# A hybrid decoder block on one core: the first loads cut into smaller pieces, the first projection by k tile, later constants

## The chip, the cores and the metric

The kernel runs on one core of one Trainium2 chip. The metric is device time in microseconds (us), from the first to the last instruction of a launch and what lies around them. Before the change the median of three runs is 2488.16 us (2482.79 to 2489.18).

## What is computed

One decoder block over 16 learned meta tokens and 512 tokens of width 2048, all in float32:

- n = RMSNorm(h), with h the meta tokens and x one after the other.
- proj = n @ w_in, 7200 columns: q, k, v, gate z, decay and write-strength columns of a gated delta rule (8 heads of 128), and q, k, v, gate, gate-rank columns of gated linear attention (4 heads).
- q, k, v of the delta rule go through a causal convolution over 4 tokens (conv_w) and SiLU; then both attentions, each with its own norm and gate.
- h = h + mixed @ w_out; h = h + (silu(n2 @ w_gate) * (n2 @ w_up)) @ w_down; a final RMSNorm; the meta tokens are dropped.

## The kernel before, in words

**Dense products.** They are a stream of granules of weights. A granule of w_in is 4 k tiles (of 128 rows) by 256 columns, 512 KB. It is loaded into a tile `raw` (2 buffers), split by ScalarE into a high part `wh` (a cast to float32r) and by VectorE into a low part `wl` = raw - wh (3 buffers each), and used in 8 units. A unit (`unit` in `job`, line 450) is one k tile by 128 columns: six products of 258 or 264 columns, high by high, high by low, low by high, for two halves of the tokens. Four granules (16 k tiles) are one projection of 256 columns; its two times two results stay in four banks of PSUM (`psD`, 4 buffers) until they are scaled by R1 (1 / the norm of each token) on VectorE. The first projection is the queries of heads 0 and 1. In a granule all four k tiles of the first 128 columns come before those of the second.

**The stream.** `run_granules` (line 252) splits granule i+1 and issues loads up to granule i+3 at the head of granule i, then issues the units; after unit 0 (after unit 5 while the start's `hooks` last) it splits granule i+2. The weight loads are issued from ScalarE's queue, but the first two from SyncE's (lines 1551, 1553).

**The start.** SyncE loads x in 16 pieces of 128 tokens by 512 columns (256 KB), with the first two granules of weights between them. ScalarE's queue loads the rows of three weight vectors into `rowsA` (lines 290 to 292: attn_norm_w, ffn_norm_w, conv_w) and the meta tokens (line 294). TensorE runs nine products of ones (`warm`), transposes `rowsA`, and VectorE copies the result to `colA`, which holds the norm's weights by column (`aw`, `fw`) and the taps of the convolution. `n_tile(k)` (line 409) transposes a k tile of x with four TensorE transposes; ScalarE writes its high part, scaled by `aw`, VectorE the low part. `n_meta` does that for all k tiles of the meta tokens. Tiles 0 to 3 and `n_meta` come ahead of the first unit; tiles 4 to 15 are hooks, one after every second unit, and between them hooks with the squares of x and the meta tokens on ScalarE (20 of them), from which R1 is made. The hook after the last of these, `start`, comes after unit 24 of the first projection: it issues the sums, `t_norm` (R1: VectorE sums, ScalarE roots, a VectorE product, two TensorE products, a VectorE copy), `t_consts` (masks, then seven small loads on SyncE's queue, a transpose, the flag "consts") and the tasks of the four pairs of heads.

**The work beside the products.** Every engine runs in the order of the text. Convolutions, attentions and gates are generators cut into steps (`tick`, `step`, lines 152 to 167); a step is issued between two units once, by the kernel's own rough count of nanoseconds (`Paced`, `clock`), what the step before has issued is done. So a task that starts later falls between other units. `t_conv` (line 608) begins when its projection's flag is set, with a ScalarE product by a column of `colA`. A pair of heads (`t_pair`, line 651) solves its triangular blocks on VectorE with tiles `bl` and `y`; `y` is loaded from a small DRAM tile `idd` by three SyncE loads (line 738), and `need` (line 176) is what the stream calls when it can't go on without a flag.

Of the kernel before, what the change touches and what calls it, by code (L numbers as in the profile page):

```python
# [59 lines left out]
class Clock:  # L60
    """where the engines stand by a rough count (ns) of what has been issued to them"""
    now = 0.0    # TensorE
    last = None  # the engine of the last instruction
    dma = 0.0    # transfers of the current step
    chain = 0.0  # end of what the current step has issued, as if each instruction waited for the one before


class Paced:
    """an engine whose instructions are counted"""
# [28 lines left out]
def tile_block(  # L98
# [47 lines left out]
    # Engines run in the order of this text: work beside the dense products is cut into steps  # L146
    # (generators) that are issued between units of the dense products, once what the step before
    # has issued is done, and while the other engines keep up.
# [28 lines left out]
    def need(ok):  # L177
        """what the dense products cannot go on without"""
        stop = clock.now + 1e6
        while not ok():  # L180
            assert clock.now < stop
            clock.now += 200
            tick()

    hooks = []  # steps of the start, one after each unit
# [6 lines left out]
    def free(n):  # L192
        """the last use of n tiles of the arena has been issued"""
        live[0] -= n

    def room(n, spare):
        """tiles of the arena for a step; the dense products keep some spare"""
        while live[0] + n > AR - spare:
            yield
# [7 lines left out]
    def acquire(tag, n=1):  # L207
        """tiles that are held across steps: at most n holders at a time"""
        while held.get(tag, 0) >= n:
            yield  # L210
        held[tag] = held.get(tag, 0) + 1
# [5 lines left out]
    # granule: (loads [(weights AP, first column of the tile)], k tiles, columns, units, after)  # L217
# [17 lines left out]
    def split(i):  # L235
        grow(i)
        while state["split"] <= min(i, len(granules) - 1):
# [4 lines left out]
            if "split" in g:  # L242
                g["w"] = g["split"](raw)
                continue
            last_split()
# [6 lines left out]
    def run_granules(a, b):  # L252
        for i in range(a, b):
            g = granules[i]
            split(i + WB - 2)
            fetch(i + WB + RAW - 2)
            for n, u in enumerate(g["units"]):
                u(*g["w"])
                clock.chain = clock.now
                if n == (5 if hooks else 0):  # L260
# [29 lines left out]
    A.dma_start(out=rowsA[96:112], in_=attn_w.rearrange("o (r c) -> (o r) c", c=P))  # L290
    A.dma_start(out=rowsA[112:128], in_=ffn_w.rearrange("o (r c) -> (o r) c", c=P))
    A.dma_start(out=rowsA[0:96], in_=conv_w.rearrange("o i (t c) -> (o i t) c", c=P))
    for g in range(2):
        A.dma_start(out=mt[g][0:NM], in_=meta[:, 1024 * g:1024 * g + 1024])
    aw = colA[:, 96:112]
# [3 lines left out]
    # more constants, off the critical path  # L299
# [14 lines left out]
    def t_consts():  # L314
# [8 lines left out]
        # persistent: the columns that no product fills stay zero  # L323
# [3 lines left out]
        def blocks(dst, step, w):  # L327
            """dst[p, n, :] = 1 for step * n <= p < step * n + w"""
# [8 lines left out]
        # score masks of the hierarchical levels: columns of the right halves alone  # L337
# [3 lines left out]
        V.memset(rowsB, 0.0)  # L341
        SP.dma_start(out=rowsB[0:1], in_=gdn_w)
# [4 lines left out]
        # rows 3i + g of the identity for row group g, the same for every block  # L347
# [4 lines left out]
        PE.transpose(out=cps[:, 0:P], in_=rowsB, identity=ident)  # L352
        V.tensor_copy(out=colB, in_=cps[:, 0:8])
        flags.add("consts")

    def rstd_of(dst, ssq, n):
        """dst = (ssq / n + eps) ** -0.5"""
# [3 lines left out]
    def row_bcast(*jobs):  # L361
        """dst[128, t n] = the columns [n, t] along the free axis, on every partition"""
# [27 lines left out]
    def load_x(g):  # L390
        for t in range(NT):
            SP.dma_start(out=xq[g][t], in_=xv[:, t, 512 * g:512 * g + 512])
# [48 lines left out]
    w_in_v = w_in[0].rearrange("(k p) c -> p k c", p=P)  # L441

    def job(loads, evac, full=True, cols=256, mw=P, kk=4, after=None, mid=None, begin=None, hv=None):
        """projection of cols columns; evac(ct, psum AP, token slice); after(), mid() once the last, the
        lower k tiles are done"""
# [23 lines left out]
        for g in range(KT // kk):  # L469
            granules.append(dict(  # L470
                loads=[(w_in_v[:, kk * g:kk * g + kk, c0:c0 + w], c) for c0, w, c in loads], kk=kk, cols=cols,
                units=[unit(ct, kk * g + i, i) for ct in range(nct) for i in range(kk)],
# [20 lines left out]
    def ab_job():  # L493
        """32 columns: the high and the low parts of the weights side by side, rows 0-31 and 32-63 of abT"""
# [69 lines left out]
    def t_silu(t, w):  # L564
        """t * sigmoid(t), sigmoid(t) = exp(min(t, 0) - log(1 + exp(-|t|))): one table set, no overflow"""
# [14 lines left out]
    def squares(t, w):  # L580
        """t * t as a pair of float32r tiles that add up to it"""
# [11 lines left out]
    def gdn_job(j, gi):  # L593
# [9 lines left out]
        # the convolution of the first query reaches back to token NM - 3; float32r products take even columns  # L603
# [4 lines left out]
    def t_conv(j, gi, h, res):  # L608
        """conv + silu of a head's q, k or v; q and k normalized as well; no query of a meta token is asked for"""
        t = 8 * gi + 2 * j + h  # L610
        yield from until(("pre", j, gi))
# [1073 lines left out]
```

## Time and profile before

| | us |
|---|---|
| median of 3 runs | 2488.16 |
| lowest, highest run | 2482.79, 2489.18 |
| span of the profiled execution (core 0) | 2485.6 |
| TensorE busy in it | 2435.0 (98%) |
| VectorE busy | 1581.9 (64%) |
| ScalarE busy | 992.4 (40%) |

The profile is one execution of the same program. Its page gives busy times and the chain of work that ended last; the trace behind it can be asked for waits (who waited for whom), for busy times in stretches, and for the instructions in order of time. A row of the timeline shows start, duration, engine, operation, output and inputs, the number of like instructions that are merged, and in brackets how long the engine sat idle before and what ended that. PE is TensorE, DVE VectorE, ACT ScalarE, SP SyncE; ACTq and SPq are the queues from which they issue transfers.

### The profile page before, as it was taken

The page shows a single profiled execution, that of the slowest core. Times are in us where ns is not written, and L with a number is a line of the kernel's source. Part 1 is how long each engine was busy: PE and PEld are TensorE (multiplying, and loading weights), DVE is VectorE, ACT ScalarE, POOL GpSimd, SP SyncE. Part 2 cuts the span into 40 slices and gives each one's busy share as a digit, 9 for nine tenths or more (in the row PEclk, how much of TensorE's full clock was granted, in tenths as well). Part 3 has the DMA queues.
Part 4 walks back from the last instruction along what each step waited for, and adds up shares of the span by engine and source line. Part 5 has one row for each costly group of instructions (what it writes and reads, how often), then busy time and mean ns, then how long its engine had stood idle before and what let it go on. Part 6 is the DMA issues. An engine that isn't in the chain of part 4 may idle for free.

```text
span 2485.6 us, 39777 instructions
## 1 busy us (share of the span) xinstructions
PE 2435.0 (98%) x16512; PEld 2249.4 (90%) x16512; DVE 1581.9 (64%) x2598; ACT 992.4 (40%) x1515; POOL 129.3 (5%) x220
## 2 busy tenths in 40 slices
PE   9989898999999999999999999999999999999998
PEld 8989898788899888889999999999999988888887
DVE  5567566647544555369888888888888854334344
ACT  6545342533343554344444444444444433222213
POOL 1011110112202100000000000000000000000000
PEclk9999999899999999999999999999999999999999
DMA  4322232222222246343333333334334475434321
GB/s 144 87 79 79 66 81 64 73 71 78 56 61 69 78 143 200 122 136 111 117 122 120 118 120 119 119 111 126 113 119 125 126 257 183 130 96 144 106 81 68
DMA packets 237412, 274.43 MB, mean 110 GB/s; under 512 B 32625, under 2 KB 180344, under 8 KB 237104
## 3 DMA queue, kind: packets, MB, share of 16 engines
q10 hardware_dynamic: 198256, 232.49, 30.6%
q1 hardware_dynamic: 38976, 39.42, 5.0%
q8 instruction: 129, 2.11, 0.4%
q14 instruction: 51, 0.42, 0.1%
HBM read 246.61 MB, written 25.25 MB: 109 GB/s over the span
## 4 chain that ended last, share of the span: by engine, by line
PE 90%; SPq 3%; DMA 3%; DVE 2%; ACT 1%; issue 0%; ACTq 0%; DVEq 0%
PE ub L92 35%; PE dn L92 21%; PE dwn L92 19%; PE wo L92 7%; SPq L92 3%; PE sc L92 1%; DMA dy<-y 1%; PE py L92 1%; DVE acc L92 1%; DMA y<-idd 1%; PE hT L92 1%; PE lo L92 1%; PE pk L92 1%; DMA raw<-in_w_in_dram 1%; PE pz L92 1%
## 5 line engine op out<-in xcount | busy, mean ns | idle before, releaser
L92 PE MATMUL ub<-pl,sh 128*128 128x256 f32 x2816 | 550.6, 282 | 0.0
L92 DVE TENSOR_TENSOR wl<-raw,wh 128x1024 fp32r<-128x1024 f32 x224 | 275.6, 1230 | 372.9 <-ACT wh L92 371.5
L92 PEld LDWEIGHTS ub<-pl,sh 128*128 128x128 f32 x2816 | 436.9, 191 | 0.6 <-issue 0.5
L92 PE MATMUL ub<-pl,ah 128*128 128x256 f32 x2112 | 424.0, 282 | 0.0
L92 ACT CAST wh<-raw 128x1024 fp32r<-128x1024 f32 x224 | 234.9, 1049 | 416.6 <-PE dwn L92 212.4
L92 PE MATMUL ub<-pl,sl 128*128 128x256 f32 x1408 | 397.6, 282 | 0.0
L92 PE MATMUL dwn<-wh,pl 128*128 128x512 f32 x1280 | 396.0, 390 | 0.0
L92 PEld LDWEIGHTS ub<-pl,ah 128*128 128x128 f32 x2112 | 327.4, 191 | 0.0
L92 PE MATMUL dn<-nA,wh 128*128 128x264 f32 (+2 forms) x1472 | 304.4, 321 | 0.0
L92 PE MATMUL ub<-pl,al 128*128 128x256 f32 x1056 | 298.2, 282 | 0.0
L92 PE MATMUL dn<-nB,wh 128*128 128x264 f32 (+2 forms) x1472 | 296.4, 314 | 0.4 <-DVE nB L92 0.3
L92 PEld LDWEIGHTS dwn<-wh,pl 128*128 128x128 f32 x1280 | 240.2, 188 | 52.0 <-DVE pl L92 0.3
L92 ACT CAST sh<-us 128x1024 fp32r<-128x1024 f32 x176 | 185.0, 1051 | 237.3 <-DVE us L92 234.3
L92 PEld LDWEIGHTS ub<-pl,sl 128*128 128x128 f32 x1408 | 268.2, 190 | 0.0
L92 PE MATMUL dwn<-wl,pl 128*128 128x512 f32 x640 | 249.9, 390 | 0.0
L92 ACT CAST ah<-raw 128x768 fp32r<-128x768 f32 x176 | 147.3, 837 | 228.9 <-PE ub L92 223.1
L92 PEld LDWEIGHTS dn<-nA,wh 128*128 128x128 f32 x1472 | 223.2, 194 | 15.9 <-issue 3.2
L92 PEld LDWEIGHTS dn<-nB,wh 128*128 128x128 f32 x1472 | 218.2, 189 | 14.2 <-issue 1.2
L92 DVE TENSOR_TENSOR sl<-us,sh 128x1024 fp32r<-128x1024 f32 x176 | 214.6, 1219 | 1.8 <-ACT sh L92 1.8
L92 PEld LDWEIGHTS ub<-pl,al 128*128 128x128 f32 x1056 | 201.2, 191 | 0.0
L92 PE MATMUL dn<-nA,wl 128*128 128x264 f32 (+2 forms) x736 | 183.4, 313 | 0.0
L92 PE MATMUL dn<-nB,wl 128*128 128x264 f32 (+2 forms) x736 | 180.4, 309 | 0.0
(286 smaller groups left out, 3281.1 us busy)
## 6 DMA issues: line engine op xcount, KB each, us to landing
raw<-in_w_in_dram ACTq DMA_DIRECT2D x110, 512.0 KB
raw<-in_w_gate_dram ACTq DMA_DIRECT2D x88, 512.0 KB
raw<-in_w_up_dram ACTq DMA_DIRECT2D x88, 512.0 KB
raw<-in_w_down_dram ACTq DMA_DIRECT2D x80, 512.0 KB
raw<-in_w_out_dram ACTq DMA_DIRECT2D x32, 512.0 KB
actd<-up SPq DMA_DIRECT2D x22, 512.0 KB
jk<-actd ACTq DMA_DIRECT2D x41, 256.0 KB
x<-in_x_dram SPq DMA_DIRECT2D x16, 256.0 KB
```

Source lines behind the costliest of these rows:

```text
L92: return f(*args, **kw)
```

## The change

- The rows of attn_norm_w go alone into a tile `rowsC` of 16 rows, first on ScalarE's queue; a transpose of 16 rows gives `aw`, which is now a tile of its own. ffn_norm_w and conv_w are loaded into `rowsA` in `t_consts`, on SyncE's queue, and transposed there beside `rowsB`; `colA` is complete only then, and `t_conv` waits for "consts".
- The first 512 columns of x are loaded as two halves of 256 columns: first the four left halves, then the four right ones. The first granule of weights goes to ScalarE's queue, behind the meta tokens, as two loads of 2 k tiles. The second granule comes on SyncE's queue after the right halves, ahead of the rest of x.
- The first granule is split k tile by k tile (`split0`): k tiles 0 and 1 ahead of the first unit, 2 and 3 as hooks (in place of the squares after tiles 2 and 3).
- `n_meta` comes before tile 0; only tiles 0 and 1 come ahead of the first unit, tiles 2 and 3 are hooks. With 28 hooks ahead of it in place of 24, `start` comes after unit 28.
- In the four granules of the first projection both halves of the columns of a k tile come one after the other.
- In granule 0 the split of granule 1 comes before the hook of unit 4 and the loads of granules 2 and 3 before that of unit 5, in place of the head of the granule.
- Comments are dropped.

```diff
 run_granules:
-            split(i + WB - 2)
-            fetch(i + WB + RAW - 2)
+            first = i == 0 and len(hooks) > 0
+            if not first:
+                split(i + WB - 2)
+                fetch(i + WB + RAW - 2)
             for n, u in enumerate(g["units"]):
                 u(*g["w"])
                 clock.chain = clock.now
-                if n == (5 if hooks else 0):
+                if first:
+                    if n == 4:
+                        split(i + WB - 2)
+                    if n == 5:
+                        fetch(i + WB + RAW - 2)
+                elif n == (5 if hooks else 0):
                     split(i + WB - 1)
 constants:
-    A.dma_start(out=rowsA[96:112], in_=attn_w...)
-    A.dma_start(out=rowsA[112:128], in_=ffn_w...)
-    A.dma_start(out=rowsA[0:96], in_=conv_w...)
-    for g in range(2):
-        A.dma_start(out=mt[g][0:NM], in_=meta[...])
-    aw = colA[:, 96:112]
+    rowsC = const.tile([16, P], F32, name="rowsC")
+    aw = const.tile([P, 16], F32, name="aw")
 t_consts:
         V.memset(rowsB, 0.0)
+        V.memset(rowsA, 0.0)
+        SP.dma_start(out=rowsA[112:128], in_=ffn_w...)
+        SP.dma_start(out=rowsA[0:96], in_=conv_w...)
...
         PE.transpose(out=cps[:, 0:P], in_=rowsB, identity=ident)
+        PE.transpose(out=cps[:, P:2 * P], in_=rowsA, identity=ident)
         V.tensor_copy(out=colB, in_=cps[:, 0:8])
+        V.tensor_copy(out=colA, in_=cps[:, P:2 * P])
         flags.add("consts")
 job:
-                units=[unit(ct, kk * g + i, i) for ct in range(nct) for i in range(kk)],
+                units=[unit(ct, kk * g + i, i) for ct in range(nct) for i in range(kk)] if len(granules) >= KT // kk
+                else [unit(ct, kk * g + i, i) for i in range(kk) for ct in range(nct)],
 t_conv:
+        yield from until("consts")
         yield from until(("pre", j, gi))
 issue:
-        load_x(0)
-        fetch(0, SP)
-        load_x(1)
-        fetch(1, SP)
+        grow(0)
+        g0 = granules[0]
+        raw0 = g0["raw"] = wp.tile([P, 4, 256], F32, name="raw", tag="raw", bufs=RAW)
+        g0["w"] = w0h, w0l = [...]
+        state["dma"] = 1
+        A.dma_start(out=rowsC, in_=attn_w...)
+        load_x(0, 0, 256)
+        for g in range(2):
+            A.dma_start(out=mt[g][0:NM], in_=meta[...])
+        w0v = g0["loads"][0][0]
+        for i in range(2):
+            A.dma_start(out=raw0[:, 2 * i:2 * i + 2, :], in_=w0v[:, 2 * i:2 * i + 2, :])
+        def split0(i):
+            A.copy(out=w0h[:, i, :], in_=raw0[:, i, :])
+            V.tensor_tensor(out=w0l[:, i, :], in0=raw0[:, i, :], in1=w0h[:, i, :].bitcast(F32), op=ALU.subtract)
+        load_x(0, 256, 512)
+        fetch(1, SP)
+        load_x(1)
         load_x(2)
         load_x(3)
...
-        PE.transpose(out=cps[:, 0:P], in_=rowsA, identity=ident)
-        V.tensor_copy(out=colA, in_=cps[:, 0:P])
-        for k in range(2):
-            n_tile(k)
-        split(0)
+        PE.transpose(out=cps[:, 0:16], in_=rowsC, identity=ident[0:16, 0:16])
+        V.tensor_copy(out=aw, in_=cps[:, 0:16])
+        split0(0)
         n_meta()
-        for k in range(2, 4):
-            n_tile(k)
+        n_tile(0)
+        split0(1)
+        n_tile(1)
...
-        for k in range(4, KT):
+        for k in range(2, KT):
             hooks.append(lambda k=k: n_tile(k))
-            hooks.append(lambda n=2 if k < 12 else 1: [squares...])
+            if k < 4:
+                hooks.append(lambda k=k: split0(k))
+            else:
+                hooks.append(lambda n=2 if k < 12 else 1: [squares...])
```

## Rows read from the trace of the kernel before

**Rows 1.** The page: span, then busy us (share of the span) and instructions.
```profile
span 2485.6 us, 39777 instructions
PE 2435.0 (98%) x16512; PEld 2249.4 (90%) x16512; DVE 1581.9 (64%) x2598; ACT 992.4 (40%) x1515; POOL 129.3 (5%) x220
```
**Rows 2.** PE's waits, whole span: who for whom, us in total, times, longest.
```profile
PE py L92 <- DVE z L92: 15.9, 2, 9.6
PE lg L92 <- DMA w2h<-in_gla_gate_w_dram: 8.4, 1, 8.4
PE l L92 <- ACT sqH L92: 7.0, 1, 7.0
```
**Rows 3.** DVE's waits from 150 to 600 us, same columns.
```profile
DVE tmp L92 <- DMA y<-idd: 27.2, 3, 10.5
...
DVE tmp L92 <- DMA w2h<-in_gla_gate_w_dram: 11.8, 1, 11.8
```
**Rows 4.** Timeline of SyncE's queue, 384 to 404 us.
```profile
385.80 14.58 SPq L92 DMA_DIRECT2D y<-idd  x3
```
**Rows 5.** Stretches: PE, PEld, DVE, ACT, POOL busy (instructions), granted clock, DMA, GB/s.
```profile
50.00:75.00 25.00, 25.00 (x204) 24.54 (x204) 15.88 (x26) 15.18 (x25) 0.00 (x0) 1.00 0.33 74
75.00:100.00 25.00, 24.23 (x200) 23.59 (x198) 15.56 (x33) 15.23 (x26) 2.75 (x6) 1.00 0.31 87
175.00:180.00 5.00, 4.91 (x21) 4.81 (x22) 4.90 (x11) 1.96 (x3) 0.00 (x0) 0.50 0.22 79
```
**Rows 6.** Timeline of PE, 0 to 48 us.
```profile
1.70 4.21 PE L92 MATMUL warm<-ones_w,onesR 128*128 128x512 f32 x9 [1.70 <-DVE ones_w L92]
6.88 0.45 PE L92 MATMUL cps<-ident,rowsA 128*128 128x128 f32 x1 [0.97 <-DMA rowsA<-in_gdn_conv_w_dram]
...
10.40 1.03 PE L92 MATMUL mps<-ident,nt 16*128 16x16 f32 x8 [0.41 <-DMA nt<-in_meta_tokens_dram]
...
12.99 1.21 PE L92 MATMUL dn<-nA,wh 128*128 128x258 f32 x4
...
14.42 1.06 PE L92 MATMUL xT<-ident,x 128*128 128x128 f32 x4
15.13 1.21 PE L92 MATMUL dn<-nA,wh 128*128 128x258 f32 x4
...
17.56 0.60 PE L92 MATMUL xT<-ident,x 128*128 128x128 f32 x4
...
18.74 0.65 PE L92 MATMUL dn<-nA,wh 128*128 128x258 f32 x4
...
19.47 0.60 PE L92 MATMUL xT<-ident,x 128*128 128x128 f32 x4
...
42.01 0.36 PE L92 MATMUL rb<-dg,onesR 16*128 16x16 f32 x2 [0.47 <-DVE dg L92]
...
46.42 0.64 PE L92 MATMUL dn<-nA,wh 128*128 128x264 f32 x4
```
**Rows 7.** Timeline of VectorE, around 12 us and 44 us.
```profile
11.86 0.42 DVE L92 TENSOR_TENSOR mtmp<-mps,colA 128x256 f32<-128x256 f32 x1
...
44.47 0.76 DVE L92 TENSOR_TENSOR pre<-dn,R 128x258 f32<-128x258 f32 x2
```
**Rows 8.** Timeline of ScalarE, 12 to 50 us.
```profile
12.31 0.30 ACT L92 CAST nA<-mtmp 128x128 fp32r<-128x128 f32 x1 [1.63 <-DVE mtmp L92]
...
16.98 0.69 ACT L92 ACTIVATE nA<-xT,colA 128x512 fp32r<-128x512 f32 x1 [1.73 <-DVE wl L92]
...
40.16 0.20 ACT L92 ACTIVATION_READ_ACCUMULATOR sg<-x 128x1 f32 x1
...
49.85 1.33 ACT L92 ACTIVATE acc<-pre,colA 128x512 f32<-128x512 f32 x2
```
**Rows 9.** The first 6 us as one stretch, columns as in rows 5.
```profile
0.00:6.00 6.00, 4.21 (x9) 2.81 (x9) 0.78 (x5) 1.28 (x1) 5.04 (x23) 1.00 0.62 186
```
**Rows 10.** Timeline of PE, 64.5 to 66 us: the transpose of the later constants.
```profile
65.17 0.27 PE L92 MATMUL cps<-ident,rowsB 128*128 128x128 f32 x1
```

More of the change, by code (lines that the diff above doesn't have):

```diff
@@ L244, in split @@
                 continue
+            if "w" in g:
+                continue
             last_split()
@@ L289, in tile_block @@
     mt = [mx.tile([P, 4, 2, P], F32, name="nt", tag="nt", bufs=2).rearrange("p a b c -> p (a b c)") for _ in range(2)]
-    A.dma_start(out=rowsA[96:112], in_=attn_w.rearrange("o (r c) -> (o r) c", c=P))
-    A.dma_start(out=rowsA[112:128], in_=ffn_w.rearrange("o (r c) -> (o r) c", c=P))
-    A.dma_start(out=rowsA[0:96], in_=conv_w.rearrange("o i (t c) -> (o i t) c", c=P))
-    for g in range(2):
-        A.dma_start(out=mt[g][0:NM], in_=meta[:, 1024 * g:1024 * g + 1024])
-    aw = colA[:, 96:112]
+    rowsC = const.tile([16, P], F32, name="rowsC")
+    aw = const.tile([P, 16], F32, name="aw")
     fw = colA[:, 112:128]
@@ L341, in t_consts @@
         V.memset(rowsB, 0.0)
+        V.memset(rowsA, 0.0)
+        SP.dma_start(out=rowsA[112:128], in_=ffn_w.rearrange("o (r c) -> (o r) c", c=P))
+        SP.dma_start(out=rowsA[0:96], in_=conv_w.rearrange("o i (t c) -> (o i t) c", c=P))
         SP.dma_start(out=rowsB[0:1], in_=gdn_w)
@@ L388, in tile_block, with load_x @@
     xq = [[ta(f"x{g}_{t}", 512) for t in range(NT)] for g in range(4)]
-    def load_x(g):
+    def load_x(g, a=0, b=512):
         for t in range(NT):
-            SP.dma_start(out=xq[g][t], in_=xv[:, t, 512 * g:512 * g + 512])
+            SP.dma_start(out=xq[g][t][:, a:b], in_=xv[:, t, 512 * g + a:512 * g + b])
     def n_meta():
@@ L1549, in tile_block @@
     with tc.manual_schedule():
-        load_x(0)
-        fetch(0, SP)
+        grow(0)
+        g0 = granules[0]
+        raw0 = g0["raw"] = wp.tile([P, 4, 256], F32, name="raw", tag="raw", bufs=RAW)
+        g0["w"] = w0h, w0l = [wp.tile([P, 4, 256], F32R, name="w" + q, tag="w" + q, bufs=WB) for q in "hl"]
+        state["dma"] = 1
+        A.dma_start(out=rowsC, in_=attn_w.rearrange("o (r c) -> (o r) c", c=P))
+        load_x(0, 0, 256)
+        for g in range(2):
+            A.dma_start(out=mt[g][0:NM], in_=meta[:, 1024 * g:1024 * g + 1024])
+        w0v = g0["loads"][0][0]
[6 more added lines that the diff above has]
+        fetch(1, SP)
         load_x(1)
-        fetch(1, SP)
         load_x(2)
@@ L1563, in tile_block @@
         cps = pm("cps")
-        PE.transpose(out=cps[:, 0:P], in_=rowsA, identity=ident)
-        V.tensor_copy(out=colA, in_=cps[:, 0:P])
-        for k in range(2):
-            n_tile(k)
-        split(0)
+        PE.transpose(out=cps[:, 0:16], in_=rowsC, identity=ident[0:16, 0:16])
+        V.tensor_copy(out=aw, in_=cps[:, 0:16])
+        split0(0)
         n_meta()
-        for k in range(2, 4):
-            n_tile(k)
+        n_tile(0)
+        split0(1)
+        n_tile(1)
         squares_left = [lambda g=g, t=t: x_sq(g, t) for g in range(4) for t in range(NT)]
         squares_left[8:8] = [lambda g=g: m_sq(g) for g in range(4)]
-        for k in range(4, KT):
+        for k in range(2, KT):
             hooks.append(lambda k=k: n_tile(k))
-            hooks.append(lambda n=2 if k < 12 else 1: [squares_left.pop(0)() for _ in range(n) if squares_left])
+            if k < 4:
+                hooks.append(lambda k=k: split0(k))
+            else:
+                hooks.append(lambda n=2 if k < 12 else 1: [squares_left.pop(0)() for _ in range(n) if squares_left])
         def start():
```

## The prediction

> **What bounds the kernel now.** The page comes first: TensorE is busy 2435.0 of 2485.6 us [rows 1], so all that can be won by moving work about is some 50 us, and the question is where they lie. The table of TensorE's waits answers it for the named ones [rows 2]: 15.9 + 8.4 + 7.0 = 31.3 us in four long waits, none of them at the start. VectorE's waits show their common cause [rows 3]: four times VectorE stands still for the solver's tile, 27.2 us in three waits for `y<-idd`, and 11.8 us before the fourth solve, put down to a load that was queued behind the same transfers. The queue's own row shows why: the three `y` loads of a pair occupy SyncE's queue for 14.58 us [rows 4]. Everything in order behind VectorE then stops TensorE. After such a wait TensorE also runs slower: 21 matmuls in 5 us at a granted clock of 0.50, which is the 1.2 GHz level, after an idle stretch, where a full stretch has 204 in 25 us, or 41 in 5 us [rows 5]. That is about 2.4 us lost for each wait, on top of it.
>
> Then the start, which is what the diff edits. TensorE warms up from 1.70 to 5.91, waits for `rowsA` until 6.88, and makes its first real product at 12.99; the second projection's first product is at 46.42 [rows 6]. What the change can win must show up before that last time.
>
> **What limits 13 to 46 us.** TensorE's pace at full speed is one transpose tile and two units in 19.47 - 17.56 = 1.91 us; a transpose alone takes about 0.47 of it and a unit 0.72. Before about 16.5 us the same forms are half as fast (four products in 1.21 us at 12.99 and 15.13, in 0.65 at 18.74; four transposes with 1.06 at 14.42, 0.60 at 17.56) [rows 6]: the 1.2 GHz level, although the granted clock prints 1.00 for the first 6 us [rows 9] with their equally slow warm-up (4.21 us for nine products of 512 columns).
>
> ScalarE is just as full. From tile 4 at 16.98 to the last square at 40.16 it does 12 tiles, 20 squares and 3 casts of weights in 23.2 us [rows 8], and I find no gap in that stretch of its timeline. R1 hangs on that last square: its first TensorE product comes 1.85 us later, at 42.01, after TensorE has waited for it [rows 6], and the first results have left PSUM at 44.47 + 0.76 = 45.23 [rows 7]. So 42.01 to 45.23, 3.2 us, is the fixed tail behind ScalarE's chain.
>
> **The change part by part, the start.**
>
> 1. *First product.* The constants needed first are 8 KB where they were 64 KB, and the first x pieces are half as long. In the first 6 us 0.186 MB per us came in, 1.12 MB in all [rows 9]; the new first needs (x halves 0.52 MB, meta 0.13, half a granule 0.26, rowsC) are 0.92 MB, so they can be there by about 5.5 to 6 us, when the warm-up ends anyway (5.91). Then in a chain: transpose of `rowsC`, 0.2 (bounded by the 0.45 of the old one); 16 meta transposes, two groups of 1.03; VectorE's `mtmp` 0.43 after them (10.40 + 1.03 to 11.86); ScalarE's first meta cast 0.45 after that (12.31), two casts, 0.6; tile 0 on ScalarE 0.69. 5.91 + 0.2 + 2.06 + 0.43 + 0.45 + 0.6 + 0.69 = 10.3 us, against 12.99 [rows 6 to 8]. 2.7 us are won here, if nothing behind gives them back.
>
> 2. *Tiles 2 and 3 move behind the first unit.* Before, they were done ahead of it. ScalarE's tile 4 now comes after five units and three transpose tiles of TensorE. At full speed these are 2.5 x 1.91 + 0.24 = 5.0 us, plus 0.5 for ScalarE's turn: 15.8 us. If the clock rises at 16.5 as before, only 3.1 us of that work is done by then and tile 4 comes at about 18.9. Against 16.98 this is between 1.2 earlier and 1.9 later.
>
> 3. *ScalarE's chain behind it* is the same 23.2 us. The wait of 1.73 us for the low part of granule 1's weights, ahead of tile 4 before [rows 8], comes behind it now (the two weight loads are queued on ScalarE's own sequencer after unit 5, the second one until VectorE has read `raw`); between 0 and 1.73, I take 0.7, because the split is issued one unit sooner. The last square is then at 15.8 + 23.2 + 0.7 = 39.7 to 42.8 us, before 40.16.
>
> 4. *Split by k tile.* Four casts of 256 columns in place of one of 1024: two lie ahead of the first unit in ScalarE's idle time before the meta casts (1.63 us idle there [rows 8]), two in its idle time before tiles 3 and 4. No price while TensorE is the slower one there; else below 0.7, inside the ends of step 2.
>
> 5. *Order by k tile, `start` after unit 28.* R1's products now stand behind unit 30 and not 27, so TensorE has 3 x 0.72 = 2.2 us more before it needs R1. But the next projection follows one unit later and needs the banks that R1 has yet to clear; before, four units lay between. So the second projection starts when the first results are out: last square + 1.85 + 3.2, that is 44.8 to 47.9 us, against 46.42. By its own pace TensorE is there earlier.
>
> The sum of the start: between 1.6 us earlier and 1.5 later. I take 46.3, the middle, or 0.1 us earlier: nearest to the old row, since both ends come from the same chain on ScalarE. In short, the 2.7 us won at the first product are spent waiting for ScalarE.
>
> A rule bears on the two ends. The Trainium skill, "TensorE: Matmul & The Clock Gate", section "What's actually happening", says that the array's clock is set by how busy the engine has lately been; by it earlier work with fewer gaps brings the rise forward, and the sum would go to 44.8. By the rows, where nine products without a gap did not raise it [rows 6], it would go to 47.9.
>
> **The change part by part, afterwards.**
>
> 6. *Late constants.* The convolution of the first queries began on ScalarE at 49.85 [rows 8]. It now waits for the transpose of the constants, at 65.17 before [rows 10]; `start` is 4 units later (2.9 us) and two more loads are counted ahead of it (about 1 us in the kernel's count), so it begins near 69 us, some 20 us later. Behind it wait two convolutions, which now run beside those of the keys. From 75 to 100 us ScalarE and VectorE are busy 15.23 and 15.56 of 25 us [rows 5], so there is room for most of them. I price it at nothing: the cover is this idle time. If the cover is gone, weights are split late, and TensorE pays up to the overflow: 15.18 + 15.23 - 25 = 5.4 us if all of ScalarE's work of 50 to 75 had to move, 0 if none.
>
> 7. *SyncE's queue.* The two new loads in `t_consts` stand ahead of five others, on a queue that is idle then; nothing but "consts" waits for them. Two transposes and one copy of 128 columns more: 0.3 us of TensorE [rows 10], given back by the shorter transpose at the start.
>
> 8. *Another order of steps.* From there on, steps fall between other units. The four solves keep their loads; how long TensorE waits in each depends on how many split weights lie ahead. I take no change, and keep the ends for the rivals.
>
> The profiled span is 2485.6 us, 2.6 below the median of the runs shown, and within their spread; the difference is added to the median. 2488.16 - 0.1 is 2488.0 us.
>
> **The rivals.**
>
> - *One solver wait goes or shrinks (faster).* For: the waits differ already (7.0 to 9.6 us), so position matters. Against: all four hang on the same queue occupancy of 14.58 us, which stays. One wait less is worth 7.0 + 2.4 to 9.6 + 2.4 us: 2476.0 to 2478.6.
> - *The solver waits lose their cover (slower).* Place: the four solves. VectorE stands 27.2 + 11.8 = 39.0 us in the waits named, TensorE 31.3 [rows 2, 3]: 7.7 us are hidden by weights split ahead. Late convolutions (step 6) crowd VectorE and ScalarE before the first solves, so fewer lie ahead. Price: the whole 7.7, to 10.1 with one more slow stretch of 2.4: 2495.7 to 2498.1. It decides from the point where no split granule is left when the load is awaited. Against: the convolutions of the first pair have some 40 us to catch up.
> - *The whole 2.7 us arrive.* That needs ScalarE to keep pace in units 0 to 30. Its 23.2 us without a gap speak against it. 2485.3 us.
> - *The pieces land no earlier,* because both queues feed the same transfers and x's halves share with meta and weights. Then the first product stays near 13 us and the bank wait of step 5 is added, about 1 us: 2489 us.
>
> **How the numbers follow.** About 0.3%, 7.5 us, is what a measurement of this kernel can tell from no change. The forecast has 0.58, the whole gain 0.08 and no earlier landing 0.05, all within 7.5 us: same 0.71. A wait that goes has 0.16 (faster), cover that is lost 0.13 (slower). The range: the forecast's own is 2486.5 to 2489.7 from the ends of the start, and up to 2495 with the overflow of step 6. With most of the two outer cases it is 2476 to 2497, which leaves out less than 2 in 10.
>
> **What would show it.** Right: first product between 10 and 11 us; ScalarE full from tile 4 to the last square; a wait of TensorE of about 1 us for the first banks at the start of the second projection, which begins between 44.8 and 47.9 us; the first convolution near 69 us; four waits for `y` of some 6 to 10 us. Wrong: a second projection starting before 44, a gap on ScalarE's timeline between tile 4 and the last square (step 3), TensorE waiting for weights between 70 and 115 us (step 6), or a sum of the solver's waits off by more than 7 us (step 8).

## The result and the profile after

The changed kernel takes 2502.68 us (median of 5 runs, 2501.70 to 2506.75), the kernel before 2488.78 (5 runs): ratio 1.0066, 95% interval 1.0056 to 1.0077. It is **slower**, by 13.9 us in the medians and by 18.3 us in the two profiled executions (2503.9 and 2485.6 us), and it lies above the range of the prediction. Numbers read from the two traces add up to the larger figure. The medians of the kernel before lie between 2486.97 and 2488.78 in all comparisons below.

The page, beside [rows 1]; TensorE is just as full:

```profile
span 2503.9 us, 39773 instructions
PE 2443.7 (98%) x16513; PEld 2255.9 (90%) x16513; DVE 1580.7 (63%) x2603; ACT 991.2 (40%) x1518; POOL 129.2 (5%) x220
```

**Where the time came in.** The output projection (`wo`) follows all input projections. Its row in the kernel before, then in the changed one (min/median/max ns, first and last start):

```profile
L92 PE MATMUL wo<-wh,mH x256: 387/392/479, 920.6 to 1107.4; 128*128 128x512 f32 x128
```
```profile
L92 PE MATMUL wo<-wh,mH x256: 389/393/479, 939.4 to 1126.1; 128*128 128x512 f32 x128
```

It starts 18.8 us late and lasts as long as before: all of the loss between the two traces lies ahead of 939 us.

**The start.** TensorE's timeline of the changed kernel, beside [rows 6]:

```profile
7.48 0.66 PE L92 MATMUL mps<-ident,nt 16*128 16x16 f32 x8 [0.61 <-DMA nt<-in_meta_tokens_dram]
8.08 1.09 PE L92 MATMUL xT<-ident,x 128*128 128x128 f32 x8
...
10.95 1.58 PE L92 MATMUL dn<-nA,wh 128*128 128x258 f32 x4 [1.78 <-ACT nA L92]
...
27.62 0.51 PE L92 MATMUL dn<-nA,wh 128*128 128x258 f32 x2 [2.00 <-ACT nA L92]
...
47.30 0.36 PE L92 MATMUL rb<-dg,onesR 16*128 16x16 f32 x2
...
50.24 0.97 PE L92 MATMUL dn<-nA,wh 128*128 128x264 f32 x4 [0.53 <-DVE pre L92]
```

ScalarE's timeline, beside [rows 8]:

```profile
8.58 0.40 ACT L92 CAST wh<-raw 128x256 fp32r<-128x256 f32 x1 [6.50 <-DMA raw<-in_w_in_dram]
...
17.10 0.69 ACT L92 ACTIVATE nA<-xT,aw 128x512 fp32r<-128x512 f32 x1 [2.26 <-PE xT L92]
...
18.99 0.69 ACT L92 ACTIVATE nA<-xT,aw 128x512 fp32r<-128x512 f32 x1
...
20.80 0.63 ACT L92 ACTIVATE sg<-x 128x512 f32<-128x512 f32 x1 [1.12 <-DVE wl L92]
...
26.45 0.38 ACTq L92 DMA_DIRECT2D raw<-in_w_in_dram  x1
26.88 0.69 ACT L92 ACTIVATE nA<-xT,aw 128x512 fp32r<-128x512 f32 x1 [1.71 <-DVE wl L92]
...
45.46 0.19 ACT L92 ACTIVATION_READ_ACCUMULATOR sg<-x 128x1 f32 x1
```

The first product comes 2.0 us earlier (10.95 for 12.99), and the second projection 3.8 us later (50.24 for 46.42). ScalarE begins the squares at 20.80 and ends them at 45.46 (40.16 before). At 26.45 it issues the load of the fifth granule, which may only go once VectorE has read the buffer; ScalarE is idle for 1.71 us there, the next tile is late, and TensorE waits 2.00 us for it at 27.62. The granted clock (the third column from the end) of the first stretches with products:

```profile
10.00:15.00 5.00, 4.05 (x17) 0.50 1.02 378
15.00:20.00 5.00, 5.00 (x37) 0.83 0.78 279
```

**Behind the start** another 15 us come in (18.8 less 3.8). The named waits of TensorE, beside [rows 2], hardly show them:

```profile
PE l L92 <- DVE sqL L92: 12.0, 2, 11.2
PE po L92 <- DVE vn L92: 8.3, 2, 8.0
PE pv L92 <- ACT vt L92: 7.8, 2, 5.5
PE sc L92 <- DVE nt L92: 7.6, 1, 7.6
```

That is 35.7 us in four rows, for 31.3 in three. The first pair of heads, though, is late. Its first product with the decays (`pe`), before and after (first and last start):

```profile
L92 PE MATMUL pe<-g,suR x10: 172/280/285, 111.8 to 145.0; 128*128 128x256 f32 x8, 16*16 16x32 f32 x2
```
```profile
L92 PE MATMUL pe<-g,suR x10: 173/279/284, 135.7 to 175.1; 128*128 128x256 f32 x8, 16*16 16x32 f32 x2
```

It is 23.9 us late where the stream of dense products is 4. And the stream has two holes that it did not have. Busy time of the dense products (`dn`) alone, in stretches of 20 us (then their number, granted clock, DMA, GB/s), before and after:

```profile
300.00:320.00 20.00, 15.69 (x61) 1.00 0.27 75
320.00:340.00 20.00, 18.37 (x121) 1.00 0.30 84
...
400.00:420.00 20.00, 11.33 (x74) 0.76 0.15 43
420.00:440.00 20.00, 17.11 (x122) 1.00 0.28 81
```
```profile
300.00:320.00 20.00, 12.30 (x84) 0.83 0.16 41
320.00:340.00 20.00, 4.34 (x30) 0.77 0.13 44
...
400.00:420.00 20.00, 6.19 (x24) 0.99 0.31 84
420.00:440.00 20.00, 7.83 (x42) 0.59 0.09 30
```

The edges of the holes on TensorE's timeline of the changed kernel:

```profile
324.87 0.40 PE L92 MATMUL dn<-nB,wl 128*128 128x258 f32 x2
...
340.63 1.23 PE L92 MATMUL dn<-nA,wh 128*128 128x264 f32 x4
...
407.28 0.40 PE L92 MATMUL dn<-nB,wl 128*128 128x512 f32 x1
...
424.33 0.79 PE L92 MATMUL po<-pt,vn 128*128 128x128 f32 x2 [7.97 <-DVE vn L92]
...
431.46 1.23 PE L92 MATMUL dn<-nA,wh 128*128 128x264 f32 x4
```

From 325.3 to 340.6 and from 407.7 to 431.5, 15.4 and 23.8 us, no dense product runs. TensorE is not simply idle in them: it runs the small steps of the pairs, one after another, with waits between them (the longest 7.97 us) and partly at the lower clock. The inside of both holes, columns as in [rows 5]:

```profile
326.00:340.00 14.00, 10.16 (x55) 9.45 (x54) 10.54 (x43) 2.27 (x8) 1.69 (x5) 0.67 0.00 1
410.00:430.00 20.00, 9.72 (x58) 8.82 (x56) 8.72 (x32) 4.18 (x11) 0.10 (x1) 0.74 0.09 27
```

TensorE is busy for 10.16 of 14 us and for 9.72 of 20. So the table of waits misses much of the loss. All stretches over 6 us without a dense product, from the timelines: before 9.1, 9.3, 12.7, 9.6, each just after the load of `y` for one of the four pairs; after 12.0, 7.2, 15.4, 23.8, 9.3.

### The profile page after: what moved, and what is told of

It is laid out like the page before. It is cut to its first block, busy times and chain, and to the rows that moved or that the text cites. A ratio compares the mean times of both kernels' runs of the same rounds, so it can differ in the third digit from the quotient of the medians.

```text
span 2503.9 us, 39773 instructions
## 1 busy us (share of the span) xinstructions
PE 2443.7 (98%) x16513; PEld 2255.9 (90%) x16513; DVE 1580.7 (63%) x2603; ACT 991.2 (40%) x1518; POOL 129.2 (5%) x220
## 4 chain that ended last, share of the span: by engine, by line
PE 91%; SPq 3%; DMA 2%; DVE 2%; ACT 1%; issue 1%; ACTq 0%; DVEq 0%
PE ub L92 35%; PE dn L92 22%; PE dwn L92 19%; PE wo L92 7%; SPq L92 3%; PE sc L92 1%; PE py L92 1%; DMA dy<-y 1%; PE po L92 1%; DMA y<-idd 1%; PE hT L92 1%; PE pz L92 1%; PE pk L92 0%; PE lo L92 0%; DMA yc<-dy 0%
## 5 line engine op out<-in xcount | busy, mean ns | idle before, releaser
L92 DVE TENSOR_TENSOR wl<-raw,wh 128x1024 fp32r<-128x1024 f32 (+1 forms) x227 | 276.4, 1218 | 403.9 <-ACT wh L92 402.3
L92 ACT CAST wh<-raw 128x1024 fp32r<-128x1024 f32 (+1 forms) x227 | 235.2, 1036 | 445.1 <-PE dwn L92 203.8
```

What stands on the lines that cost most here:

```text
L92: return f(*args, **kw)
```

## The experiments

The first four runs asked whether the loss comes from the late constants, from the start, or from any new order.

**1. The wait alone.** Before, with one line:

```diff
 t_conv:
+        yield from until("consts")
         yield from until(("pre", j, gi))
```

> The kernel before with one line added: the convolutions wait for the flag that the late constants set, though their own constants are there early; the start is not touched. Theory (late convolutions): the first pair's first decay product moves from 111.8 to 125 to 135 us, pair after pair runs late, the output projection starts at 930 to 936 us instead of 920.6, and the time is 2498 to 2503 us. Rival 'the head' (the new order of the start costs it all): no change, output projection at 920 +- 2, time 2487 to 2491 us. Rival 'redraw' (any shift of the planner's steps throws the solver waits anew): no fixed value, anywhere from 2478 to 2503, and not tied to how late the pairs are.

Measured: 2498.74 us, ratio 1.0048 (1.0033 to 1.0063), 11 us slower. The start is the old one (second projection at 46.12). First decay product and output projection:

```profile
L92 PE MATMUL pe<-g,suR x10: 173/279/283, 131.2 to 170.6; 128*128 128x256 f32 x8, 16*16 16x32 f32 x2
L92 PE MATMUL wo<-wh,mH x256: 387/392/479, 933.8 to 1120.6; 128*128 128x512 f32 x128
```

Both are in the expected places. The holes are there too, 15.4 us at 319.6 and 24.0 at 402.0. One wait for a flag, with no load, product or copy moved by the text, makes some three quarters of the loss. The first convolution is only 8.2 us later than before (58.07 for 49.85), the pair 19.4.

**2. Early constants in the changed kernel.** `rowsA` is loaded behind the x pieces and transposed in `start`; the wait goes.

```diff
 issue:
         load_x(3)
+        V.memset(rowsA, 0.0)
+        SP.dma_start(out=rowsA[112:128], in_=ffn_w...)
+        SP.dma_start(out=rowsA[0:96], in_=conv_w...)
 start:
             free(16)
+            cA = pm("cps")
+            PE.transpose(out=cA[:, 0:P], in_=rowsA, identity=ident)
+            V.tensor_copy(out=colA, in_=cA[:, 0:P])
 t_consts:
-        V.memset(rowsA, 0.0)
-        SP.dma_start(out=rowsA[112:128], in_=ffn_w...)
-        SP.dma_start(out=rowsA[0:96], in_=conv_w...)
...
-        PE.transpose(out=cps[:, P:2 * P], in_=rowsA, identity=ident)
-        V.tensor_copy(out=colA, in_=cps[:, P:2 * P])
 t_conv:
-        yield from until("consts")
```

> The changed kernel with the convolution's constants loaded at the start again (behind the x pieces, on SyncE's queue), transposed when R1's steps are started, and no wait for the late constants in the convolutions. The start is otherwise the changed one. Theory (late convolutions): about 4 us of the start's loss stay, the rest goes: second projection at 50, first convolution taps at about 55 us, output projection at 923 to 928 us, time 2490 to 2495 us. Rival 'the head': nothing comes back, output projection at 936 to 940, time 2500 to 2505 us. Rival 'redraw': anywhere from 2478 to 2505, with solver waits that don't follow the pairs' lateness.

Measured: 2491.66 us, ratio 1.0015 (1.0005 to 1.0025): 11 us of the medians come back and 4 stay, as the theory had it. The late holes are gone (four stretches, 9.6, 9.2, 12.2, 9.5 us). So the loss has two parts that add: some 4 us from the start, some 11 from the constants. One number missed: the output projection begins at 928.7, not 923 to 928; in this profile the second projection starts at 51.69.

**3. The start's blocked load.** The fifth granule's load goes from the head of granule 1 to behind its fourth unit.

```diff
 run_granules:
                 split(i + WB - 2)
-                fetch(i + WB + RAW - 2)
+                if i > 1:
+                    fetch(i + WB + RAW - 2)
...
+                elif i == 1 and n == 3:
+                    fetch(i + WB + RAW - 2)
```

> The changed kernel with the load of the fifth granule of weights issued after the fourth unit of the second granule instead of ahead of its first. Theory: ScalarE's sequencer no longer stands 1.7 us for VectorE's low parts at 26.9 us, TensorE's wait of 2.0 us for a tile of the normed input goes, the second projection starts 1 to 2.5 us earlier (47.7 to 49.2 instead of 50.2), and the time falls by no more than that: 2499 to 2503 us. Rival 'the head' (the start carries the whole loss): 2488 to 2496 us. Rival 'redraw': moves by more than 5 us in either direction.

Measured: 2502.28 us, ratio 1.0064 (1.0049 to 1.0079), no gain. The wait of 1.71 us on ScalarE is gone, and from its first cast to its last square it takes 34.8 us instead of 36.9; but in this execution that first cast came at 10.47 instead of 8.58, and the second projection starts at 50.09, not at 47.7 to 49.2. So this run can't tell what a mended start is worth.

**4. Another draw of the order.** Before, with one constant of the planner's count:

```diff
-SEM_NS = 140
+SEM_NS = 150
```

> The kernel before with one constant of the planner's count, the cost of a hop between engines, at 150 instead of 140 ns: no work is added or moved by the text but by the order that the planner draws from it. Rival 'redraw': the time moves by 8 us or more in either direction, the solver waits by as much. Theory (late convolutions): the pairs start within 3 us of before, and the time stays within 5 us of before, 2484 to 2494 us.

Measured: 2502.45 us, ratio 1.0061 (1.0046 to 1.0076): 15 us slower, with no work added. Here my theory failed: an order alone can cost as much as the change. But the draw is not free either. The first decay product is late in this kernel too (128.8 for 111.8), and the long hole is there (23.7 us at 401.0). What the three slow kernels share is a late first pair and these holes.

**The new theory: the arena is full.** Convolution inputs, outputs and gates live in an arena of 21 tiles. A projection may begin only when its two (or four) tiles are free (`room_now`, which calls `need`: no dense unit is placed until then). Late pairs give their tiles back late, while the stream goes on. The kernel's own count of nanoseconds, by which it places its steps, says where the stream stands for room and for how long in that count (it is not a measurement):

```
kernel                        stands (us of the kernel's count)
before                        none
late constants put back (2)   none
the change                    13.9 at k3, 16.0 at v3
the wait alone (1)            13.9 at k3, 16.0 at v3
hop at 150 ns (4)              9.7 at k3, 16.6 at v3
the change, 22 tiles           2.7 and 6.4, at two later jobs
hop at 150 ns, 22 tiles       none
before, 20 tiles               3.8, 10.3, 1.2, 1.7, at later jobs
```

k3 and v3 are the keys and values of the fourth pair (the next expectation gives them other names). They are the two holes of the timeline: 340.63 is the first product of k3, 431.46 that of v3.

**5. One tile more in the changed kernel.** `rowsC` moves into the unused half of the tile of `rowsA`, which makes the room.

```diff
-AR = 21
+AR = 22
-    rowsC = const.tile([16, P], F32, name="rowsC")
+    rowsC = rowsA_tile[0:16, P:2 * P]
```

> The changed kernel with 22 tiles in the arena instead of 21 (the rows of the first constants share the unused half of another tile, which makes the room). New theory (full arena): the late first pair holds its tiles longer, the dense stream runs ahead of the pairs until the arena is full, at the sixth job of keys and at the first GLA job, and stands there while only the pairs' serial steps run. By the kernel's own count the two stands are 13.9 + 16.0 us with 21 tiles and 0 there (2.7 + 6.4 later) with 22; in the trace the pairs stay as late as in the changed kernel (first decay product at 130 to 138 us), but the job k3 no longer begins with a hole at 325 to 343 us, the output projection starts at 925 to 932 us and the time is 2488 to 2496 us. Rival 'crowding and solver waits' (late convolutions take the engines, the queue does the rest): one tile more changes nothing, 2499 to 2505 us.

Measured: 2492.43 us, ratio 1.0022 (1.0012 to 1.0032): 10 us come back. The constants are as late as in the changed kernel, and so is the pair; the dense products fill the holes (rows as above):

```profile
L92 PE MATMUL pe<-g,suR x10: 173/281/288, 137.3 to 176.6; 128*128 128x256 f32 x8, 16*16 16x32 f32 x2
```
```profile
300.00:320.00 20.00, 8.28 (x54) 0.83 0.13 33
320.00:340.00 20.00, 13.94 (x100) 1.00 0.18 53
...
400.00:420.00 20.00, 15.09 (x108) 1.00 0.28 80
420.00:440.00 20.00, 11.11 (x58) 0.91 0.28 84
```

The longest stretch without a dense product is 11.2 us, and the output projection starts at 922.6, sooner than expected. Crowded engines do not care for a tile more; that rival is out.

The late pair also changes the order of the jobs: `z0`, the gate of the first pair, is drawn once that pair is far enough. Its first result (`zt`) leaves the banks at 325.8 us before, ahead of the queries and keys of the fourth pair, and at 404.0 after the change, behind them. Kernel 5 keeps the changed order there (`zt` at 385.7, behind k3) and still wins its 10 us, so it is the stands and not this order that cost them. One control is missing: the kernel before with 22 tiles was not run. Kernel 6 is the nearest to it.

**6. One tile more for the other draw.** Kernel 4 with `AR = 22`.

> The kernel before with the planner's hop at 150 ns (which cost 15 us) and 22 tiles in the arena. Theory (full arena): with 21 tiles the kernel's own count has stands of 9.7 + 16.6 us at the same two jobs as the changed kernel, with 22 it has none; so the loss goes: output projection at 918 to 926 us, 2484 to 2492 us. Rival 'redraw' (each order has its own luck): anything from 2480 to 2503 us.

Measured: 2484.70 us, ratio 0.9991 (0.9982 to 1.0000): the 15 us that kernel 4 had lost are back and 3 more, with the pair as late (129.9) and the output projection at 918.0. The "redraw" was the same full arena. Here `z0` also moves ahead of k3, so stands and order change together; and that a 22nd tile wins a few us without any stand is not excluded: this kernel is 2.8 us faster than the kernel before.

**7 and 8. The solver's transfers.** The rival of the prediction was that the solver's waits lose their cover. Here the transfers that make these waits are taken away, in the kernel before and in the changed one:

```diff
 t_consts:
+        for g in range(3):
+            SP.dma_start(out=y0[34 * g:34 * g + 34], in_=idd...)
 t_pair:
-        for g in range(3):
-            SP.dma_start(out=y[34 * g:34 * g + 34], in_=idd...)
+        G.tensor_copy(out=y, in_=y0)
```

> The kernel before with the solver's start values kept in a tile of their own, loaded once, and copied by GpSimd for each pair in place of the three DMA loads. All theories: VectorE's waits for y<-idd (27.2 us in three) go, TensorE's waits behind them fall from 31 us to some 5 to 15, and the time falls to 2462 to 2480 us. It is the base for the next run.

> The changed kernel with the same copy of the solver's start values. Theory (full arena): the stands at the two jobs are still in the kernel's own count (13.9 + 16.2 us), so it stays 8 to 18 us slower than the kernel before with the copy. Rival 'solver waits lose their cover' (as the prediction had it): with the solver's transfers gone the two differ by no more than the start's 2 to 4 us.

Measured: 2471.43 us (0.9938, 0.9918 to 0.9958) and 2481.85 (0.9982, 0.9972 to 0.9991). Both win, and 10.4 us stay between them: the holes at k3 and v3 are still there (15.3 and 17.8 us). The solver's waits are a cost of their own, not the cause; they are shorter now, not gone. In place of 14.58 us on the queue for each pair [rows 4] stand 0.47 on GpSimd, and VectorE's first wait in the solver is now for `bl`:

```profile
L92 POOL COPY y<-y 102x352 f32<-102x352 f32 x4 | 1.9, 474 | 0.0
```
```profile
DVE tmp L92 <- DMA bl<-dn: 17.5, 4, 6.2
```

17.5 us in four, for 27.2 in three [rows 3].

**9. The start mended.** Kernel 2 with the edit of kernel 3, with metas and tile 0 ahead of the first cast of weights on ScalarE, and with four squares beside the casts of the third and fourth k tile.

```diff
-        split0(0)
         n_meta()
         n_tile(0)
-        split0(1)
+        split0(0)
         n_tile(1)
+        split0(1)
...
-                hooks.append(lambda k=k: split0(k))
+                hooks.append(lambda k=k: (split0(k), [squares_left.pop(0)() for _ in range(2)]))
```

> The changed kernel with the early constants of the second run, and its start mended at three places: the fifth granule's load after the fourth unit of the second granule; ScalarE casts the metas and tile 0 ahead of the first part of the weights; four of the squares are issued beside the casts of the first granule's third and fourth k tile, where ScalarE stood idle for 2.1 and 2.3 us. Theory (the start's loss is ScalarE's chain, idle at 12 to 17 us and blocked at 26.9 us): the last square comes at 40.5 to 43 us instead of 45.5, the second projection starts at 45 to 48 us instead of 50.2 to 52, no stand for the arena, time 2484 to 2489 us. Rival (the order by k tile itself, or the first loads, cost the start): second projection still at 49.5 or later, time 2490 to 2494 us as with the early constants alone.

Measured: 2488.55 us, ratio 1.0006 (0.9997 to 1.0015), inside the expected time, but the place was wrong: the last square comes at 38.26, earlier than expected, and R1 does not follow it.

```profile
38.26 0.18 ACT L92 ACTIVATION_READ_ACCUMULATOR sg<-x 128x1 f32 x1
...
43.16 0.69 ACT L92 ACTIVATE nB<-xT,aw 128x512 fp32r<-128x512 f32 x1 [0.80 <-PE xT L92]
45.12 0.30 ACT L92 ACTIVATE rs<-rs,eps_c 128x4 f32<-128x4 f32 x1 [1.27 <-DVE ssm L92]
```

R1's root stands behind the last x tile (43.16, waiting for TensorE), since `start` comes after unit 28 in the order of the text. The second projection starts at 49.43, not at 45 to 48. ScalarE's chain was one limit of the start; the place of the last tile and of `start` is a second one, almost as late.

**10. Those and the solver's copy together.**

> The same with the solver's start values copied on the chip. It joins what the runs so far support: no late constants, mended start, no transfers for the solver. Expected from the kernel before with the copy (2471.4) and the mended start (0 to 3 us better than before): 2467 to 2473 us; if the parts don't add, because the stream now runs ahead of the pairs again, 2475 or more.

Measured: 2467.07 us, ratio 0.9924 (0.9908 to 0.9941): the parts add.

**11. One tile fewer, before.** `AR = 20`, nothing else.

> The kernel before with 20 tiles in the arena. Theory (full arena): the kernel's own count has stands of 3.8 + 10.3 + 1.2 + 1.7 us where it had none, so it should be 6 to 15 us slower: 2493 to 2503 us, with pairs that start where they did before (first decay product at 110 to 114 us). Rival 'lateness of the pairs itself': no change, 2485 to 2490 us, as the pairs are on time.

Measured: 2537.27 us, ratio 1.0203 (1.0188 to 1.0218). The pairs are on time (first decay product at 111.2), so lateness alone is not the cause; but the loss is 50 us and not 6 to 15, and it lies elsewhere. The output projection starts at 922.0, on time, and is starved afterwards (TensorE's busy time, granted clock):

```profile
900.00:950.00 50.00, 38.79 (x195) 0.83 0.24 74
950.00:1000.00 50.00, 43.31 (x173) 0.79 0.30 94
```

Before, both stretches are full at 1.00. The trace shows what is left for the end. Between 928.5 and 974.0 us no product of the output projection runs; TensorE runs the products of the last head of gated linear attention instead. Their rows before and in this kernel:

```profile
L92 PE MATMUL lo<-lq,lS x64: 270/275/275, 623.4 to 858.7; 128*128 128x128 f32 x64
```
```profile
L92 PE MATMUL lo<-lq,lS x64: 270/275/580, 741.7 to 968.4; 128*128 128x128 f32 x64
```

The first head's products start 118 us later, and the last head's end 47 us after the output projection has begun. A head waits for four free tiles before its first product (`room(4, ...)` in `t_gla`, line 973), and in the kernel's own count the first head waits 122 us there, where it did not wait before. So the arena has no tile to spare, but here the side work pays for the missing one and not the stream, and the count of the stream's stands gave the wrong price. The order of the jobs changes too, since the draw looks at the free tiles.

**12. Tiles 2 and 3 ahead of the first unit again.** Kernel 9, with every x tile made eight units ahead of its use instead of four, so that the last tile and `start` come four units earlier (after unit 24, as before the change); the constants' transpose comes behind R1's first steps in `start`.

```diff
         n_tile(1)
         split0(1)
+        n_tile(2)
+        n_tile(3)
...
-        for k in range(2, KT):
+        for k in range(4, KT):
```

> As the run with the mended start, but with x tiles 2 and 3 transposed ahead of the first unit again, so that each tile is made eight units ahead of its use instead of four; the transpose of the convolution's constants comes behind R1's first steps instead of ahead of them. Theory (the order by k tile left each tile only four units, 2.9 us, for ScalarE and VectorE, and every hitch there reaches TensorE): first product 0.5 to 2 us later than 10.4, but TensorE's waits for the normed input at 20 to 30 us go, and the second projection starts at 45.5 to 48 us instead of 49.4; time 2484 to 2488 us. Rival (the start is bound by TensorE's own slow stretch at 10 to 17 us, 0.50 of the clock): 48.5 us or later, no gain.

Measured: 2486.37 us, ratio 0.9995 (0.9985 to 1.0004). The second projection, 3.9 us earlier than in kernel 9:

```profile
45.53 0.96 PE L92 MATMUL dn<-nA,wh 128*128 128x264 f32 x4 [0.53 <-DVE pre L92]
```

The rival is not settled by this run: its first product is later (11.35 for 10.42), but its slow stretch is shorter as well (granted clock 0.71 from 10 to 15 us and 1.00 from 15 to 20; in kernel 9 0.50 and 0.86). The next run settles it. The lead of the tiles, the place of `start` and the transpose were not tried apart.

**13. The same with the solver's copy.**

> The same start, with the solver's start values copied on the chip. If the eight units of lead are worth 1 to 4 us at the second projection and the order of the steps stays clear of the full arena (one stand of 1.7 us in the kernel's own count, as in the version at 2467): 2462 to 2468 us; else 2467 to 2472.

Measured: 2467.70 us, ratio 0.9922 (0.9906 to 0.9939). That lies in both expected ranges and decides nothing between them. The second projection starts at 47.12 here and at 48.15 in kernel 10; of that nothing reaches the end. In this execution TensorE is at the lower level through the whole stretch of 15 to 20 us (granted clock 0.50), where kernel 10 has 1.00:

```profile
15.00:20.00 5.00, 5.00 (x25) 0.50 0.84 287
```

Its second projection is the earlier one all the same, so the slow clock is not what holds the start. It costs something: with the same start, kernel 12 has 45.53. Kernels 10 and 13 are the best versions, 20 us faster than before and 35 faster than the change.

## Why the prediction was wrong

**Step 6 failed.** It placed the first convolution near 69 us, and it came at 69.63. It then asked one question, whether ScalarE and VectorE have idle time to catch up, and priced the delay at nothing, at most 5.4 us. The engines had the time; TensorE did not wait for weights between 70 and 115 us, so the sign that the prediction named for a failure of this step did not appear either. What had no slack was the arena: in the kernel's own count the stream never stands for room before the change and stands twice with the wait, and one tile fewer costs the kernel before 50 us. By the medians kernel 1 prices the step at 11 us, kernels 2 and 5 at 11 and 10. The work beside the products had been treated as something that may slide; it also holds what the stream needs.

**Step 8 failed with it.** "I take no change" for another order: kernel 4 shows an order that costs 15 us, and kernel 6 that it does so by the same arena.

**Step 1** came out at 10.95 for 10.3, but in part by luck. In four more executions of this start (kernels 2, 3, 5 and 8) the first product comes at 11.85, 12.83, 12.45 and 12.27; in six of the old start it comes between 12.30 and 13.17. So the gain is nearer 0.6 us, median against median, than 2.7, and those executions lie close to the rival in which the pieces land no earlier. The sum also hid two differences: the metas' products ran at the full clock (eight in 0.66 us, for the 1.03 of [rows 6]), and the second group of them waited 0.61 us for its load.

**Step 2** was right, at the later of its two ends: tile 4 at 18.99 for 18.9.

**Step 3 was mis-sized.** Its wait behind VectorE's low parts was to be 0 to 1.73 us, taken as 0.7; there are two, 1.12 and 1.71. 18.9 + 23.2 + 2.8 = 44.9, close to the 45.46 measured; it had taken 39.7 to 42.8. The rows of before showed that wait once; the edit issues the same blocked load directly behind the cast whose buffer it needs, and that could have been read off the diff.

**Step 5** had the mechanism: last square + 1.85 + 3.2 = 50.5, measured 50.24. (R1's products stand behind unit 31, and behind 28 before, not 30 and 27; the difference of three is right.) But it gave the later place of `start` no price of its own, and kernel 9 shows that it is a limit, hidden behind the first. The sum of the start, 46.3, is 3.9 us too low: 1.6 because the late end of step 2 came and not the middle, 2.1 by the waits of step 3. Kernel 2 puts the start's part of the loss at 4 us.

**Steps 4 and 7**: nothing in the traces or the runs speaks against them, though seven loads and not five stand behind the two new ones of step 7. They were not tried alone.

**The rivals.** "Solver waits lose their cover" had the sign and the first link (late convolutions of the first pair) and the wrong mechanism: the named waits grew by 4.4 us, not by 7.7, and without the transfers 10.4 us of loss stay (kernels 7 and 8). "One solver wait goes" did not happen by itself; with the transfers taken away, 16 us are won (kernel 7).

**The clock** decided which end of step 2 came. TensorE transposed at full speed at 8.08 (eight transposes in 1.09 us; four took 1.06 at 14.42 in [rows 6]), then waited 1.78 us for its first product. The granted clock of 10 to 15 us is 0.50, the 1.2 GHz level; that of 15 to 20 is 0.83, a mean over both levels. So the work up to tile 4 ran slowly, as in the prediction's later end. The Trainium skill, "TensorE: Matmul & The Clock Gate", section "What's actually happening", makes the clock depend on how busy the engine has lately been. The trace agrees: the earlier work had brought the full clock by 8.08, and it was lost again around the wait. (The same nine products of ones stand ahead of it, so that they do not raise the clock holds for the trace of before alone.) What lies above that end, 50.24 for 47.9, is ScalarE's waits of step 3.

Why 8 us of delay at the first convolution become 19 at the pair (kernel 1) is argued only: the convolutions share one scratch tile each for the SiLU and the squares (`SG`, `SQ`), so those of the queries, which ran alone before, now queue with those of the keys.

## What to carry to other kernels

Before pricing a delay of side work at nothing, ask what that work holds (tiles, banks, buffers) and who else needs it, and look at how full that pool was: what covers a delay is the scarcest of the resources, here the tiles and not the idle time of the engines. A stall for buffers may show only in part as waits, when the engine stays busy with small serial work; a table of the main stream's busy time in stretches shows it. And where an order is drawn by a rough count, change a constant of the count first: it shows how much of a difference is the draw, and here it led to the cause.

## What was not expected of the hardware

The same first loads landed at different times in different executions. ScalarE's first cast waits for the first half granule; with the same loads ahead of it, it came at 8.58 us in the changed kernel and at 10.47 in kernel 3. Gains of 1 to 2 us at the start can't be read from one profile.

GpSimd's copy of 102 x 352 values takes 0.47 us where three loads of the same values from a small DRAM tile took 14.58 on the queue. The loads themselves are not that long: kernel 7 issues the same three once, at 62 us, 3 us after the load ahead of them.

```profile
62.08 3.48 SPq L92 DMA_DIRECT2D y<-idd  x3
```

In a pair they stand right behind three loads of `bl` of 136 KB each; what holds them there was not followed. The Trainium skill, "DMA: Bandwidth & Descriptors", section "Why a DMA increments its semaphore by 16 and not by 1", says that one descriptor moves one contiguous run of the last dimension. By that, each load is 34 x 11 = 374 descriptors of 128 bytes, an estimate from the shape of the tile; their number is the same in both places, so it alone does not explain the 14.58 us.
